# Row-wise exponentials on ScalarE in the transposed blocks of a matmul-logsumexp kernel

## The chip, the cores and the metric

The kernel runs on one core of one Trainium2 chip. The metric is the device time of one execution in microseconds (us). Engines are named as in the profile: PE is TensorE's matmul, PEld its weight load, DVE is VectorE, ACT is ScalarE, POOL is GpSimd. L382 means line 382 of the kernel that was profiled; inserted lines shift the numbers between kernels.

## The reference

```python
def setup_inputs():                    # m, k, n = 1024, 4096, 4096
    return {"a": np.random.randn(m, k).astype(np.float32),
            "b": np.random.randn(k, n).astype(np.float32)}

def reference(a, b):
    x = np.matmul(a, b)
    return special.logsumexp(x, axis=-1).astype(np.float32)
```

Only the 1024 results leave the chip. The product of a and b is reduced while it is still on the core.

## The kernel before

The columns of b are worked off in eight blocks of 512. Within a block, the kernel uses seven half-size products in place of eight (a Strassen scheme), so it also needs sums of quarters of b (`t1`, `t3`, `t4`, `t6`, `t7`, made on VectorE in fp16) and sums of result tiles. Blocks 3 to 6 are "transposed" (`wide` in the code): there b is the stationary operand, the columns of b lie on the partitions, and one matmul streams 512 rows of a. Each such block has two halves, and a half consists of seven products of 16 matmuls. Block 7, which follows, is not transposed.

In a transposed result tile the logsumexp has to go over partitions. So VectorE transposes the tile in squares of 32x32. Then each partition holds, for each of 16 groups, 32 values of one row of the result, with a maximum of its own. Before the change that maximum is subtracted by VectorE over the whole tile (a broadcast addition), one ScalarE instruction takes all 512 exponentials per partition, and VectorE sums them by group:

```python
    slots = [slots[:, 0:FD], slots[:, FD : 2 * FD]]      # two scratch tiles, 128x512 fp32
    blocks32 = lambda t: t.rearrange("p (c n) -> p c n", n=32)

    def lse_turned(c, slot, h, r):
        nm = tnm[:, 1 + h, ts(r, WN // 2)]
        v = blocks32(slot)
        nc.vector.transpose(out=slot, in_=c)
        nc.vector.tensor_reduce(out=nm, in_=v, axis=AX.X, op=ALU.max, negate=True)
        add(v, v, nm.unsqueeze(-1).broadcast_to((P, WN // 2, 32)))
        nc.scalar.activation(out=slot, in_=slot, func=AF.Exp)
        return lambda: nc.vector.tensor_reduce(
            out=tts[:, 1 + h, ts(r, WN // 2)], in_=v, axis=AX.X, op=ALU.add)

    def merge_turned():      # brings the groups' sums to one common maximum
        nc.vector.tensor_reduce(out=tmin, in_=tnm.rearrange("p a c -> p c a"), ...)
        sub(tnm, tnm, tmin...)
        nc.scalar.activation(out=tnm, in_=tnm, func=AF.Exp, scale=-1.0)
        # ... a multiplication, two additions and a copy on VectorE
```

One half of a transposed block, in program order. Each engine takes its own instructions in this order. `mk` makes sums of b for the next half; in the last half before block 7 (`last`) these sums are wider.

```python
            product(c11, ..., start=True)          # product 1
            product(c12, ..., start=True)          # product 2
            product(c21, ..., start=True)          # product 3
            flush()
            nc.vector.tensor_copy(out=s[:, 1], in_=c12)   # <- the c12 copy
            add(s[:, 1], s[:, 1], c21)
            sub(s[:, 0], s[:, 1], c11)
            for f in deferred:                     # previous half's sum of c11 and merge
                f()
            deferred.clear()
            mk("t1")
            product(c22, ..., start=True, stop=True)      # product 4
            mk("t6")
            mk("t3")
            product(c12, ..., stop=True)           # product 5 ADDS INTO c12
            sub(s[:, 0], c12, s[:, 0])
            add(c22, c22, s[:, 0])
            end12 = lse_turned(c12, slots[0], 1, 0)
            end22 = lse_turned(c22, slots[1], 1, 1)
            product(c21, ..., stop=True)           # product 6
            sub(s[:, 1], c21, s[:, 1])
            end12()
            end21 = lse_turned(c21, slots[0], 0, 1)
            end22()
            # ... mk("t4"), mk("t7")
            product(c11, ..., stop=True)           # product 7
            add(c11, c11, s[:, 1])
            e = fix_pool.tile([P, FD], f32, ...)
            end11 = lse_turned(c11, e, 0, 0)
            end21()
            # ... in the last half the rest of t4 and t7
            deferred.extend([end11, merge_turned])
```

A quad of block 7 (cut), which matters at the hand-over from the last transposed half:

```python
                m1(c11, start=True)
                m5(c12)
                nc.scalar.copy(out=e, in_=halves(r0))     # first copy of block 7
                m2(c21, start=True)
                m6(c22, start=final)
            nc.scalar.copy(out=s[:, 2], in_=c21)
            flush()
            # ... add, sub
            for f in deferred:                            # the merge of the last transposed half
                f()
            # ...
            m3(c12)                                       # adds into c12: waits for the first copy
            nc.scalar.copy(out=x[:, 0], in_=c12)
            m4(c21)
            nc.scalar.copy(out=x[:, 1], in_=c21)
            m7(c11)
```

## Time and profile before

| what | before |
|---|---|
| time, median of the first 6 runs | 427.2 us (426.86 to 428.54) |
| profiled span | 426.7 us |
| the eight transposed halves | 24.17 us each, TensorE never waits |
| TensorE's one long wait (hand-over to block 7) | 6.16 us |
| the 32 matmuls after it | 5.99 us, where full clock needs 3.49 |

The page's first two parts give the busy time of each engine over the whole span, then the busy share of each of 40 slices in tenths (a 9 is 90% or more). PEclk is the granted TensorE clock in tenths.

```profile
PE 413.9 (97%) x2747; PEld 261.7 (61%) x2747; DVE 338.4 (79%) x773; ACT 83.3 (20%) x191; POOL 79.1 (19%) x149
PE   8999999999999999999999999999999958999996
DVE  2556687888566648989999999999999997299955
ACT  2222250151142211101010110101010012222124
PEclk9999999999999999999999999999999996999999
```

TensorE is full but for one dip near the end (the 5 and the 8), and the clock drops in the slice of that dip's end (the 6). VectorE is nearly full in the transposed stage (147 to 340 us), ScalarE nearly idle.

The windows view gives the busy time of each engine in a stretch of time: one of the middle halves, the last half, then the wait at the hand-over, then the 32 matmuls after it.

```profile
core 0: us, PE busy (x) PEld busy (x) DVE busy (x) ACT busy (x) POOL busy (x), PEclk, DMA share, GB/s
243.93:268.10 24.17, 24.17 (x114) 10.96 (x112) 22.91 (x50) 2.80 (x5) 1.22 (x2) 1.00 1.03 171
316.45:340.60 24.15, 24.15 (x115) 10.96 (x113) 22.95 (x45) 1.54 (x3) 2.27 (x3) 1.00 0.03 4
347.45:353.61 6.16, 0.16 (x3) 0.00 (x0) 6.02 (x11) 1.16 (x3) 0.00 (x0) 0.87 1.24 207
353.61:359.60 5.99, 5.99 (x32) 4.43 (x32) 4.40 (x13) 0.77 (x3) 0.89 (x6) 0.57 1.24 207
```

In each half TensorE is busy throughout, while VectorE is busy for 22.9 of 24.17 us. It is near its limit but does not set the period. At the hand-over VectorE works without a gap while TensorE does nothing, and the matmuls after that run at a clock of 0.57 on the mean.

The waits view of TensorE from 147 to 362 us (what it waited for, and on whom; us in total, times, longest) has only this line, and the timeline of that moment (start, duration, and in brackets the idle time before and what ended it) shows why.

```profile
PE acc_0_0_3173 L528 <- ACT s_0_3175 L595: 6.0, 1, 6.0
```

```profile
351.67 0.69 DVE L86 TENSOR_TENSOR ew_1_3155<-ew_1_3155,ident 128x512 f32<-128x512 f32 x1
352.45 0.63 ACT L381 ACTIVATE ew_1_3155<-ew_1_3155 128x512 f32<-128x512 f32 x1 [5.24 <-DVE ew_1_3155 L86]
352.99 0.57 ACT L595 COPY s_0_3175<-acc_0_0_3173 128x512 f32<-128x512 f32 x1
```

ScalarE's copy of block 7's first tile (L595) stands behind the exponential of the last transposed tile (L381), which waits 5.24 us for VectorE's broadcast addition (L86). ScalarE itself is idle all that time, but it takes its instructions in order. The Trainium skill says the same of its queue ("TensorE: Matmul & The Clock Gate", the table at its head: eight deep, strict first in, first out), and this trace agrees with the order.

### The profile page before, as it was taken

How to read it: one execution, taken by the hardware profiler on the slowest of the kernel's cores; microseconds unless marked ns; L12 is line 12 of the kernel's file. 1: busy time of each engine (PE TensorE's matmuls, PEld its weight loads, DVE VectorE, ACT ScalarE, POOL GpSimd, SP SyncE). 2: the span in 40 equal slices, each digit the busy share in tenths (PEclk: the TensorE clock that was granted, in tenths of full speed). 3: DMA queues.
4: the chain of work that ended last, by engine and by line, in shares of the span. 5: the costliest groups of instructions: out<-in, count | busy, mean ns of one | idle time of the engine just before them, and what ended most of it. 6: DMA issues, size and time to landing. Idle time of an engine off the chain costs nothing.

```text
span 426.7 us, 6832 instructions
## 1 busy us (share of the span) xinstructions
PE 413.9 (97%) x2747; PEld 261.7 (61%) x2747; DVE 338.4 (79%) x773; ACT 83.3 (20%) x191; POOL 79.1 (19%) x149
## 2 busy tenths in 40 slices
PE   8999999999999999999999999999999958999996
PEld 3555568888888844444444444444444456888885
DVE  2556687888566648989999999999999997299955
ACT  2222250151142211101010110101010012222124
POOL 7667753001020200003000300003000203220000
PEclk9999999999999999999999999999999996999999
DMA  9999999999999299008930299007940199099100
GB/s 176 202 203 203 203 206 207 207 209 211 174 175 213 39 208 170 0 2 129 208 58 0 30 207 158 2 1 120 207 68 2 17 207 173 2 170 208 20 2 1
DMA packets 57840, 53.27 MB, mean 125 GB/s; under 512 B 10192, under 2 KB 56912, under 8 KB 57808
## 3 DMA queue, kind: packets, MB, share of 16 engines
q0 software_dynamic: 48928, 49.95, 71.0%
q1 hardware_dynamic: 8880, 2.89, 4.1%
q8 instruction: 21, 0.34, 0.3%
q14 instruction: 11, 0.09, 0.1%
HBM read 100.66 MB, written 2.10 MB: 241 GB/s over the span
## 4 chain that ended last, share of the span: by engine, by line
PE 88%; DVE 6%; DMA 4%; issue 0%; ACT 0%; POOL 0%; POOLq 0%; ACTq 0%
DMA tb<-in_a_dram 3%; PE acc_1_0_1347 L528 2%; PE acc_1_0_767 L528 2%; PE acc_0_0_765 L528 2%; PE acc_3_0_3755 L528 2%; PE acc_2_0_1482 L528 2%; PE acc_1_0_3307 L528 2%; PE acc_2_0_3483 L528 2%; PE acc_3_0_1615 L528 2%; PE acc_0_0_1215 L528 2%; PE acc_3_0_3619 L528 2%; PE acc_2_0_769 L528 2%; PE wide_0_2_2823 L427 2%; PE wide_1_0_2641 L427 2%; PE wide_0_1_2470 L427 2%; PE wide_1_2_2291 L427 2%
## 5 line engine op out<-in xcount | busy, mean ns | idle before, releaser
L528 PEld LDWEIGHTS <-aT 128*128 128x128 f16 x832 | 82.7, 99 | 16.9 <-issue 6.2
L427 PEld LDWEIGHTS <-tb 128*128 128x128 f16 x384 | 37.6, 98 | 45.1
L381 ACT ACTIVATE tb<-tb 128x512 f32<-128x512 f32 x24 | 15.1, 630 | 110.4 <-DVE tb L86 110.4
L205 POOL DMA_DIRECT2D tb<-in_a_dram x47 | 25.5, 546 | 6.6 <-issue 1.2
L227 DVE COPY aT<-tps_99 128x512 f16<-128x512 f16 x24 | 10.2, 425 | 19.7 <-PE tps_99 L216 19.7
L234 PEld LDWEIGHTS <-aT 128*128 128x128 f16 x192 | 16.7, 98 | 13.8 <-DVE aT L227 1.3
L216 PEld LDWEIGHTS <-tb 128*128 128x128 f16 x192 | 14.3, 99 | 14.6 <-DMA tb<-in_a_dram 5.9
L528 PEld LDWEIGHTS <-s_71 128*128 128x128 f16 x208 | 20.4, 98 | 2.8
L528 PEld LDWEIGHTS <-s_72 128*128 128x128 f16 x208 | 20.3, 98 | 2.4
L528 PEld LDWEIGHTS <-s_73 128*128 128x128 f16 x208 | 20.3, 98 | 2.4
L229 ACT COPY aT<-tps_100 128x512 f16<-128x512 f16 x24 | 14.1, 586 | 39.0 <-PE tps_100 L216 39.0
L86 DVE TENSOR_TENSOR tb<-tb,ident 128x512 f32<-128x512 f32 x24 | 16.6, 692 | 0.8
L379 DVE TENSOR_REDUCE ident<-tb 128x16 f32<-128x512 f32 x24 | 16.5, 686 | 0.9
L382 DVE TENSOR_REDUCE tts<-tb 128x16 f32<-128x512 f32 x24 | 16.3, 678 | 0.0
L89 DVE TENSOR_TENSOR aT<-aT 128x256 f16<-128x256 f16 (+1 forms) x56 | 16.2, 343 | 0.0
L86 DVE TENSOR_TENSOR s_71<-aT 128x256 f16<-128x256 f16 (+1 forms) x26 | 8.2, 317 | 3.2 <-ACT aT L229 2.2
L216 PE MATMUL tps_99<-ident,tb 128*128 128x128 f16 x96 | 9.5, 223 | 1.0 <-DMA tb<-in_a_dram 0.8
L216 PE MATMUL tps_100<-ident,tb 128*128 128x128 f16 x96 | 9.5, 223 | 0.0
L149 POOL DMA_DIRECT2D b_0_2813<-in_b_dram x1 | 0.9, 878 | 45.1 <-DVE tb L378 45.1
L149 POOL DMA_DIRECT2D b_0_3165<-in_b_dram x1 | 0.9, 878 | 44.5 <-DVE sw_1_2997 L89 44.5
L149 POOL DMA_DIRECT2D b_0_2461<-in_b_dram x1 | 0.9, 887 | 44.4 <-PE wide_1_0_2289 L427 44.4
L149 POOL DMA_DIRECT2D b_0_2109<-in_b_dram x1 | 0.9, 878 | 44.0 <-DVE tb L378 44.0
(905 smaller groups left out, 947.5 us busy)
## 6 DMA issues: line engine op xcount, KB each, us to landing
tb<-in_a_dram POOLq DMA_DIRECT2D x47, 128.0 KB, 5.9
aT<-in_b_dram POOLq DMA_DIRECT2D x4, 1024.0 KB, 15.2
b_1_86<-in_b_dram POOLq DMA_DIRECT2D x4, 256.0 KB, 6.6
b_2_87<-in_b_dram POOLq DMA_DIRECT2D x4, 256.0 KB, 6.2
b_3_88<-in_b_dram POOLq DMA_DIRECT2D x4, 256.0 KB, 6.2
b_0_89<-in_b_dram POOLq DMA_DIRECT2D x2, 512.0 KB, 8.6
b_1_90<-in_b_dram POOLq DMA_DIRECT2D x2, 512.0 KB, 11.8
b_2_91<-in_b_dram POOLq DMA_DIRECT2D x2, 512.0 KB, 15.2
```

The source lines that it names most:

```text
L86: nc.vector.tensor_tensor(out=o, in0=x, in1=y, op=ALU.add)
L89: nc.vector.tensor_tensor(out=o, in0=x, in1=y, op=ALU.subtract)
L205: nc.gpsimd.dma_start(out=slot, in_=a_m[m, :, k0 * P : (k0 + kn) * P])
L216: nc.tensor.matmul(pst[:, ts(j, P)], src[:, ts(j, P)], ident, is_transpose=True, start=(j == 0), stop=(j == kn - 1),)
L227: nc.vector.tensor_copy(out=dst, in_=v)
L229: nc.scalar.copy(out=dst, in_=v)
L234: nc.tensor.matmul(pt, aT[:, i, kp, m // 2, m % 2, :], blk0.raw[i // GI][:, i % GI, kp, :], start=(done[m] == 0), stop=(done[m] == KT - 1),)
L379: nc.vector.tensor_reduce(out=nm, in_=v, axis=AX.X, op=ALU.max, negate=True)
L381: nc.scalar.activation(out=slot, in_=slot, func=AF.Exp)
L382: return lambda: nc.vector.tensor_reduce(out=tts[:, 1 + h, ts(r, WN // 2)], in_=v, axis=AX.X, op=ALU.add)
L427: nc.tensor.matmul(c.rearrange("p (q m) -> p q m", m=P), lhs(i), rhs(i), start=(start and i == 0), stop=(stop and i == KP - 1), skip_group ...
L528: nc.tensor.matmul(c, lhs(i), rhs(i), start=(start and i == 0), stop=(i == KP - 1), skip_group_check=True,)
```

## The change

The intent is to move work from VectorE to ScalarE. For three of the four result tiles of a half, ScalarE takes the exponentials in 16 instructions of 128x32, each with its group's maximum as the bias and with its sum accumulated on the way. VectorE loses the broadcast addition and the sum of these tiles. ScalarE also takes over the c12 copy, and this copy now stands behind the deferred work of the previous half. Lastly, in the last half, the last two of the four groups of block 7's `t1`, `t6` and `t3` are made sooner: ahead of the deferred work and the c12 copy, at a point where VectorE would otherwise wait. Three tiles are done by rows in each half, but only two in the last. The core of the diff:

```diff
-    def lse_turned(c, slot, h, r):
+    def lse_turned(c, slot, h, r, by_rows=True):
         ...
+        if by_rows:
+            for i in range(WN // 2):               # 16
+                nc.scalar.activation(
+                    out=v[:, i], in_=v[:, i], func=AF.Exp,
+                    bias=nm[:, i : i + 1],
+                    accum_out=tts[:, 1 + h, r * WN // 2 + i : r * WN // 2 + i + 1],
+                )
+            return lambda: None
         add(v, v, nm.unsqueeze(-1).broadcast_to((P, WN // 2, 32)))
 ...  (merge_turned is cut in two: up to its exponential, and the rest)
-            flush()
-            nc.vector.tensor_copy(out=s[:, 1], in_=c12)
-            add(s[:, 1], s[:, 1], c21)
-            sub(s[:, 0], s[:, 1], c11)
+            if last:
+                for what in ("t1", "t6", "t3"):
+                    for g in range(G // 2, G):
+                        mk(what, g * GI, (g + 1) * GI)
             for f in deferred:
                 f()
             deferred.clear()
-            mk("t1")
+            flush()
+            nc.scalar.copy(out=s[:, 1], in_=c12)
+            add(s[:, 1], s[:, 1], c21)
+            sub(s[:, 0], s[:, 1], c11)
+            # mk("t1"), later "t6" and "t3": whole, or in the last half only groups 0 and 1
 ...
-            end22 = lse_turned(c22, slots[1], 1, 1)
+            end22 = lse_turned(c22, slots[1], 1, 1, not last)
 ...
-            end11 = lse_turned(c11, e, 0, 0)
+            end11 = lse_turned(c11, e, 0, 0, False)
```

More of the change, by code (lines that the diff above doesn't have):

```diff
@@ L379, in lse_turned @@
         nc.vector.tensor_reduce(out=nm, in_=v, axis=AX.X, op=ALU.max, negate=True)
+        if by_rows:
+            for i in range(WN // 2):
+                nc.scalar.activation(
+                    out=v[:, i],
+                    in_=v[:, i],
+                    func=AF.Exp,
+                    bias=nm[:, i : i + 1],
+                    accum_out=tts[:, 1 + h, r * WN // 2 + i : r * WN // 2 + i + 1],
+                )
+            return lambda: None
         add(v, v, nm.unsqueeze(-1).broadcast_to((P, WN // 2, 32)))
@@ L391, in merge_turned, with merge_turned_2 @@
         nc.scalar.activation(out=tnm, in_=tnm, func=AF.Exp, scale=-1.0)
+    def merge_turned_2():
         nc.vector.tensor_mul(out=tts, in0=tts, in1=tnm)
@@ L446, in wide_step @@
             deferred.clear()
-            mk("t1")
-            product(c22, lambda i: blk.T6[:, i], lambda i: aT[:, i, 0, :, 1], start=True, stop=True)
-            mk("t6")
-            mk("t3")
+            flush()
+            nc.scalar.copy(out=s[:, 1], in_=c12)
+            add(s[:, 1], s[:, 1], c21)
+            sub(s[:, 0], s[:, 1], c11)
+            if last:
+                for g in range(G // 2):
+                    mk("t1", g * GI, (g + 1) * GI)
+            else:
+                mk("t1")
+            product(c22, lambda i: blk.T6[:, i], lambda i: aT[:, i, 0, :, 1], start=True, stop=True)
+            for what in ("t6", "t3"):
+                if last:
+                    for g in range(G // 2):
+                        mk(what, g * GI, (g + 1) * GI)
+                else:
+                    mk(what)
             product(c12, lambda i: cols(i, 0, 1), lambda i: aT[:, i, 0, :, 0], stop=True)
@@ L475, in wide_step @@
                         mk(what, g * GI, (g + 1) * GI)
-            deferred.extend([end11, merge_turned])
+            deferred.extend([end11, merge_turned, merge_turned_2])
     blk, nxt = None, blk1
```

## The prediction

> **What bounds it now.** TensorE is busy 97% of 426.7 us. From 147 to 340 us (the eight transposed half-blocks) the chain of waits is TensorE alone: seven products of 3.45 us, 24.17 us per half. In the windows by half, VectorE is busy 22.9 of 24.17 us, ScalarE only 2.8. VectorE limits only the hand-over to block 7: the last half's sums are wider (0.60 us apart instead of 0.33), VectorE runs without a gap from 327 to 352 us, ScalarE's copy of block 7's first tile queues behind the last exponential, and TensorE stands still from 347.5 to 353.6 us (its longest wait, 6.0 us). The 32 matmuls after it take 6.16 us instead of 3.49 (granted clock 0.6 in that slice). So at most 6.1 + 2.7 = 8.8 us (2.1%) can be won.
>
> **What the change does.** VectorE loses, per half, three additions (0.61 us each), three sums (0.60) and one copy with its wait (1.07): about 4.7 us. ScalarE gains that copy (0.59) and 48 exponentials of 128x32, each with a pointer bias and an accumulator read. Cost of one, estimated: in the trace, accumulating 128x256 exponentials from PSUM start their read 357 ns after they start and the next starts 92 ns later; the one from SBUF (128x257) read after 415 ns. 32 columns take 187 ns less, so 212 + 92 = about 305 ns. The Trainium skill, "ScalarE: Activation LUTs", section "What ACT_TABLE_LOAD costs", gives 280 ns + 0.833 ns per column with 93 ns overlap: 214 ns before the read, which agrees. So 16 rows cost 4.9 us where one activation cost 0.63.
>
> **Where it lands.** Busy time would fit, but the order makes a ring. The c12 copy is now behind 48 row exponentials, the last 128x512 one, and the merge's exponential. The fifth product accumulates into c12, so it must wait for that copy. Following VectorE's order: copy, 1.4 us of additions, twelve sums (4.0), subtraction, addition, transposition, maximum (2.9), then 48 x 0.305 = 14.7 on ScalarE, then last exponential, sum, minimum, subtraction, exponential, copy (about 2.7): 25.7 us, against 24.17. Replaying the old order with trace durations reproduces TensorE's resumption at 353.6; the same for the new order gives waits of about 1.5 us before the fifth product from the fourth half on, in total about 9 us, and a hand-over wait of about 4.1 instead of 6.0 us (the early sums save VectorE 3.6 us just before it). Net +7 us, less perhaps 2.7 if the shorter wait leaves the clock high.
>
> **Prediction: 431.5 us, range 422 to 439. Chances: faster by over 2% 0.04, within 2% 0.78, slower by over 2% 0.18.** A ten-nanosecond error in the row pitch moves the result by 3.2 us; below 285 ns the ring is no longer the limit.
>
> **What would show it.** Right: row exponentials about 305 ns apart; TensorE waiting 1 to 2 us per half on ScalarE's copy (c12); half periods near 25.7 us; VectorE busy under 19 us per half, now idle for ScalarE; the hand-over wait 4 us. Wrong: half periods of 24.17 us with no wait on that copy (then about 421 to 424 us), or a hand-over wait that stays at 6 us.
>
> **What would make it wrong.** A shorter row pitch because small activations pipeline better, or a longer one because accumulator reads or instruction fetches add up; a clock that drops in the new waits.

## The result

The changed kernel takes **434.78 us** (median of 10 runs, 434.14 to 436.77). The kernel before, over the 20 runs beside it, takes 427.87 us (426.86 to 428.54). The ratio is 1.0171, with a 95% interval of 1.0158 to 1.0185. A ratio here and below is the mean time of one kernel's fast runs over that of the other's in the same rounds, so it is not quite the ratio of the medians that are quoted. The result lies in the predicted range and within 2%, but the loss is about 6.9 us where the prediction had 4.3.

The page of the changed kernel, the same parts as before:

```profile
PE 412.8 (95%) x2747; PEld 260.5 (60%) x2747; DVE 303.6 (70%) x719; ACT 184.9 (43%) x912; POOL 79.1 (18%) x149
PE   7999999999999999999898998989899896999996
DVE  2566687788457845696766769666697978299865
ACT  2222250151222315829376490946829273222124
PEclk9999999999999999999999999999999998999999
```

VectorE shed 35 us and ScalarE gained 102. TensorE, which had no gap in the transposed stage, now has 8s all through it. The dip at the end became milder, both in the PE row (a 5 and an 8 before, a single 6 after) and in PEclk (from 6 to 8).

The windows view, with columns as before: one of the middle halves, the last half, then the wait at the hand-over, then the 32 matmuls after it:

```profile
246.37:272.11 25.74, 24.33 (x113) 10.93 (x112) 18.45 (x42) 16.00 (x101) 1.22 (x2) 1.00 0.97 162
323.61:349.37 25.76, 24.17 (x113) 10.83 (x111) 22.02 (x43) 16.26 (x102) 2.13 (x3) 1.00 0.02 2
356.36:360.46 4.10, 0.16 (x3) 0.00 (x0) 4.00 (x8) 3.34 (x18) 0.00 (x0) 0.92 1.24 207
360.46:365.27 4.81, 4.81 (x33) 3.74 (x32) 3.73 (x12) 0.76 (x3) 0.36 (x3) 0.72 1.24 207
```

A half now takes 25.7 us although no engine but TensorE is busy for more than 18.5 of it (22.0 in the last). So no engine's load limits it, but a chain of dependences from engine to engine does. TensorE's waits from 147 to 362 us, the first lines:

```profile
PE acc_0_0_3472 L552 <- ACT s_0_3474 L619: 3.9, 1, 3.9
PE wide_1_1_3267 L439 <- DVE tts L86: 1.6, 1, 1.6
PE wide_1_1_2407 L439 <- DVE tts L86: 1.5, 1, 1.5
PE wide_0_1_3056 L439 <- DVE tts L86: 1.4, 1, 1.4
...
```

There is one wait per half from the third half on, each time before the first matmul of the fifth product (tile `wide_..._1` is c12). The timeline of one of them shows the end of the chain:

```profile
310.09 0.31 ACT L382 ACTIVATE tb<-tb,ident 128x32 f32<-128x32 f32 x1
310.30 0.19 ACT L382 ACTIVATION_READ_ACCUMULATOR tb<-tb,ident 128x1 f32 x1
310.40 0.62 ACT L391 ACTIVATE ew_1_3042<-ew_1_3042 128x512 f32<-128x512 f32 x1
311.05 0.69 DVE L392 TENSOR_REDUCE tts<-ew_1_3042 128x16 f32<-128x512 f32 x1 [3.35 <-ACT ew_1_3042 L391]
...
312.29 0.28 ACT L401 ACTIVATE ident<-ident 128x96 f32<-128x96 f32 x1 [1.27 <-DVE ident L89]
312.47 0.57 ACT L460 COPY sw_0_3059<-wide_0_1_3056 128x512 f32<-128x512 f32 x1
...
313.09 0.38 PE L439 MATMUL wide_0_1_3056<-aT,b_0_2617 128*128 128x512 f16 x1 [1.42 <-DVE tts L86]
```

From the top: the last row exponential of c21 and its accumulator read; the exponential of c11 (L391); VectorE, which has waited 3.35 us for it, sums it (L392); the minimum and the subtraction of the merge (left out); the merge's exponential (L401); the copy of c12 (L460), ending at 313.04; and the fifth product, at 313.09. The waits view names a VectorE addition (L86) as releaser. But the trace's own record of this matmul has it wait for the counter that ScalarE's instructions raise, that is, for the copy, and experiment e1 below bears this out. The profile infers releasers from what ended nearest in time, and here it took the wrong one.

### The profile page after: what moved, and what is told of

The parts are those of the page before. It is cut to its first block, busy times and chain, and to the rows that moved or that the text cites. A ratio compares the mean times of both kernels' runs of the same rounds, so it can differ in the third digit from the quotient of the medians.

```text
span 432.3 us, 7514 instructions
## 1 busy us (share of the span) xinstructions
PE 412.8 (95%) x2747; PEld 260.5 (60%) x2747; DVE 303.6 (70%) x719; ACT 184.9 (43%) x912; POOL 79.1 (18%) x149
## 4 chain that ended last, share of the span: by engine, by line
PE 47%; DVE 25%; ACT 20%; DMA 6%; issue 1%; POOL 0%; ACTq 0%; POOLq 0%; DVEq 0%
ACT tb L382 18%; DVE tb L86 5%; DMA tb<-in_a_dram 4%; DVE ident L379 3%; DVE tb L378 3%; DVE tb L89 2%; PE acc_1_0_1347 L552 2%; PE acc_1_0_767 L552 2%; PE acc_2_0_769 L552 2%; PE acc_3_0_3918 L552 2%; PE acc_3_0_4054 L552 2%; PE acc_3_0_1615 L552 2%; PE acc_0_0_1215 L552 2%; PE acc_2_0_3782 L552 2%; PE acc_1_0_3606 L552 2%; PE acc_2_0_1482 L552 2%
## 5 line engine op out<-in xcount | busy, mean ns | idle before, releaser
L382 ACT ACTIVATE tb<-tb,ident 128x32 f32<-128x32 f32 x368 | 112.2, 307 | 72.6 <-DVE ident L379 72.6
L382 ACT ACTIVATION_READ_ACCUMULATOR tb<-tb,ident 128x1 f32 x368 | 69.0, 187 | 0.0
L86 DVE TENSOR_TENSOR s_71<-aT 128x256 f16<-128x256 f16 (+1 forms) x26 | 8.2, 316 | 1.8 <-ACT aT L229 1.5
L86 DVE TENSOR_TENSOR s_73<-aT 128x256 f16<-128x256 f16 (+1 forms) x26 | 8.3, 317 | 0.0
```

The source lines that it names most:

```text
L86: nc.vector.tensor_tensor(out=o, in0=x, in1=y, op=ALU.add)
L382: nc.scalar.activation(out=v[:, i], in_=v[:, i], func=AF.Exp, bias=nm[:, i : i + 1], accum_out=tts[:, 1 + h, r * WN // 2 + i : r * WN // 2 ...
```

## How the time divides

Profile against profile, from the start of the transposed stage to the end of the kernel:

| term | predicted | measured |
|---|---|---|
| eight halves: 193.39 to 202.89 us | about +9 | +9.50 |
| hand-over wait: 6.16 to 4.10 us | -1.9 | -2.06 |
| the 32 matmuls after it: 5.99 to 4.81 us | -2.7 | -1.19 (-0.84 in the control f1) |
| sum | +4.3 | +6.26 |

The third line is the one that failed. The part of the kernel before the stage differs between the profiles by up to about 1 us (146.22 to 147.19 us), for code that the edits don't touch, and the median of the kernel before moved from 427.2 to 427.87 us with more runs. So medians (+6.9) and profiles (+6.26) agree only that far.

## The theories

The ring theory is the prediction's. Copy of c12, two additions, twelve sums of b, a subtraction, an addition, a transposition and a maximum on VectorE, 48 row exponentials at 0.305 us on ScalarE, the last exponential, its sum, the merge up to its exponential, and the next half's copy of c12 form a ring. Its length is about 25.7 us, longer than TensorE's 24.17, because the copy was put on ScalarE behind all of this.

The load theory is the first rival: ScalarE's exponentials, or the shared memory accesses of the busier engines, slow the half wherever the copy stands.

For the hand-over the clock theory is: the wait itself costs little beyond its length, and if it gets shorter, the clock stays at full speed. The rival is that any wait of this size lowers the clock, and that behind the wait another one is hidden.

## Experiments

Diffs are against the changed kernel unless said otherwise. "Wait before the fifth product" is the sum, over the eight halves, of what a half takes beyond 24.17 us; "hand-over wait" is the time from one matmul's start to the next one's, less the 0.11 us that it is at full pace. Both are therefore 0.16 us longer for each wait than the idle time in the waits view, which begins at the modelled end of a matmul. "Left" marks what is left of the wait behind the idle matmuls; "the 32 matmuls" take 3.49 us at full clock without waits. Of f3 and g2, which are edits of the kernel before, the numbers are put beside that kernel's.

| kernel | transposed half, us | wait before 5th product | hand-over wait | the 32 matmuls | median, us | ratio to before |
|---|---|---|---|---|---|---|
| before | 24.17 | 0 | 6.16 | 5.99 | 427.87 | 1 |
| after | 25.54 to 25.92 from the third on | 9.5 | 4.10 | 4.81 | 434.78 | 1.0171 |
| e1 copy on VectorE | 24.17, last 24.67 | 0.5 | 6.20 | 5.95 | 428.44 | 1.0015 [0.999, 1.0041] |
| e2 c12 whole | 24.17 | 0 | 1.53 | 3.77 | 420.94 | 0.9843 [0.9824, 0.9863] |
| e3 c12 whole, last exp late | 24.17 | 0 | 0.13 | 5.16 | 421.13 | 0.9851 [0.983, 0.9871] |
| e4 no accumulation | 24.17, last 26.25 | 2.08 | 3.34 | 5.16 | 426.03 | 0.996 [0.9938, 0.9981] |
| f1 after again | as after | as after | 4.10 | 5.16 | 434.56 | 1.0163 [1.0134, 1.0192] |
| f2 after, idle matmuls | as after | as after | 0.61 left | 3.76 | 434.55 | 1.0158 [1.0127, 1.0188] |
| f3 before, idle matmuls | 24.17 | 0 | 0.91 left | 4.36 | 426.37 | 0.9969 [0.9944, 0.9994] |
| f4 no early sums | as after | as after | 7.71 | 4.79 | 438.75 | 1.0257 [1.0229, 1.0286] |
| g1 best | 24.17 | 0 | 0.12 | 3.49 | 419.8 | 0.9817 [0.98, 0.9833] |
| g2 f3 and merge late | 24.17 | 0 | 0.90 left | 3.49 | 425.73 | 0.9959 [0.9941, 0.9977] |
| g3 f2 and merge late | as after | as after | 0.60 left | 3.49 | 433.02 | 1.0128 [1.0113, 1.0143] |
| g4 no rows | 24.17, last 24.78 | 0.6 | 3.81 | 6.23 | 426.45 | 0.9963 [0.9941, 0.9985] |

### e1: the copy back to VectorE and, with its two additions, ahead of the merge

```diff
+            flush()
+            nc.vector.tensor_copy(out=s[:, 1], in_=c12)
+            add(s[:, 1], s[:, 1], c21)
+            sub(s[:, 0], s[:, 1], c11)
             for f in deferred:
                 f()
             deferred.clear()
-            flush()
-            nc.scalar.copy(out=s[:, 1], in_=c12)
-            add(s[:, 1], s[:, 1], c21)
-            sub(s[:, 0], s[:, 1], c11)
```

> The changed kernel with only the c12 copy put back on VectorE, ahead of the merge, as it was before; the row exponentials stay on ScalarE. Theory (ring through ScalarE's queue: copy behind 48 row exponentials): the wait before the fifth product goes, half periods return to 24.17 us although ScalarE is as busy as before (about 16 us per half); the hand-over wait is about 5.9 us; time near the kernel before, 427 to 429 us. Rival (the row exponentials themselves are too much for ScalarE, wherever the copy sits): half periods stay near 25.7 us and the time near 434 us.

The time is 428.44 us. The windows view of a half in the middle, then TensorE's waits:

```profile
242.20:266.40 24.20, 24.20 (x114) 10.94 (x112) 18.92 (x44) 15.31 (x99) 2.56 (x3) 1.00 1.06 174
```

```profile
PE acc L552 <- ACT s L619: 6.0, 1, 6.0
PE wide L439 <- DVE sw L457: 0.3, 1, 0.3
```

ScalarE still takes 48 row exponentials per half and is busy for 15.3 us, but the half takes 24.2 us again. The load theory has fallen, and the ring theory stands: the copy's place costs the 9 us. (Its engine and its position were changed together; which of the two would be enough was not tested.) The merge's VectorE additions (L86 in the waits of after) come even later than the copy in e1, and yet the fifth product waits for nobody, save 0.5 us in the last half. So it was not they that it had waited for. The hand-over wait went back to 6.2 us, 2.1 us more than in the changed kernel. Of these, 1.25 us are only that TensorE is no longer held up in the last half and so is done with it earlier (24.67 us against 25.92); the other 0.85 us are that VectorE, counted from the start of that half, takes up the last c21 tile later (29.43 us against 28.58). So a part of what the change gains at the hand-over is a wait that it has moved into the half before. (The profiled span is 0.74 us longer in its tail than before's; this is not explained.)

### e2: c12 as before, whole; c21 and c22 by rows

```diff
-            end12 = lse_turned(c12, slots[0], 1, 0)
+            end12 = lse_turned(c12, slots[0], 1, 0, False)
```

> The changed kernel with only the first of the three turned tiles (c12) going back to one addition, one whole exponential and one sum. Theory: the ring loses 4.9 - 0.6 us, falls below 24.17 us, so no wait before the fifth product; the hand-over wait falls from 3.9 to about 1.4 us; 423 us, or 420 to 421 us if the clock stays high. Rival (merging before the copy, or the early sums, make the waits): half periods stay above 25 us, time above 430 us.

The time is 420.94 us, 1.6% below the kernel before. TensorE's waits from 147 to 362 us are a single line, the hand-over:

```profile
PE acc L552 <- ACT s L619: 1.4, 1, 1.4
```

The ring has 32 row exponentials in place of 48: 16 x 0.305 = 4.9 us go from it, and one exponential of 0.63 us, with an addition and a sum on VectorE of 0.7 us each, comes in. That is enough, and TensorE doesn't wait in any half. The hand-over wait is down to 1.53 us, and the clock stays at 1.0. The remaining 0.28 us beyond 3.49 is a wait for a copy.

### e3: e2, and the last tile's exponential behind block 7's first copies

`lse_turned` gets `late`, and then issues its activation together with its sum, in the deferred part:

```diff
+        if late:
+            return lambda: (
+                nc.scalar.activation(out=slot, in_=slot, func=AF.Exp),
+                sums(),
+            )
...
-            end11 = lse_turned(c11, e, 0, 0, False)
+            end11 = lse_turned(c11, e, 0, 0, False, last)
```

> As the run before, and in the last half the exponential of c11 is issued behind block 7's two first copies on ScalarE. Theory (the hand-over wait is ScalarE's queue order, copies behind the last exponential): hand-over wait about 0, clock stays high, 419 to 420 us. Rival (block 7 waits for VectorE's sums themselves): the wait moves to another product and the time stays near that of the run before.

The time is 421.13 us, the same as e2, so the expectation was missed. The hand-over wait did go (0.13 us), but block 7's seventh product waits in its stead. The waits view, then the timeline:

```profile
PE acc L558 <- ACT s L700: 1.5, 1, 1.5
```

```profile
351.90 0.26 DVE L89 TENSOR_TENSOR ident<-ident,tmin 128x96 f32<-128x96 f32 x1
352.25 0.28 ACT L407 ACTIVATE ident<-ident 128x96 f32<-128x96 f32 x1 [3.59 <-DVE ident L89]
352.44 0.35 ACT L700 COPY s<-acc 128x256 f32<-128x256 f32 x1
352.85 0.60 PE L558 MATMUL acc<-b,aT 128*128 128x256 f16 x4 [1.50 <-ACT s L700]
```

The copy (L700) stands behind the merge's small exponential (L407), which waits for VectorE. It is the same pattern one instruction later, and it was hidden as long as the first wait was there. This is the second wait of the rival theory.

### e4: rows without the accumulation

```diff
                     bias=nm[:, i : i + 1],
-                    accum_out=tts[:, 1 + h, ...],
                 )
-            return lambda: None
+            return lambda: nc.vector.tensor_reduce(..., axis=AX.X, op=ALU.add)
```

> The changed kernel with row exponentials that take the bias but do not accumulate; VectorE makes the three sums as before. Theory (the ring's length is 48 row pitches plus 11 us): row pitch 213 ns instead of 305, ring about 21.3 us, so half periods 24.17 us (the last one about 25.6, VectorE having more to do); hand-over wait about 3.2 us; 425 to 427 us. Rival (it is the number of instructions or the position of the copy alone): half periods stay above 25 us, time 432 us or more.

The time is 426.03 us. The row exponentials now start 212 ns apart (median), against 305 ns with the accumulator read. So the read costs 93 ns per instruction in the chain, 4.5 us for 48 of them, and without it TensorE doesn't wait in seven of eight halves. (The last took 26.25 us where 25.6 were expected; the expectation puts that down to VectorE, which has more to do there. No run tests it.) The group's line of each kernel (count, busy time, mean ns of one) shows that the single instruction is no shorter, first after, then e4:

```profile
L382 ACT ACTIVATE tb<-tb,ident 128x32 f32<-128x32 f32 x368 | 112.2, 307 | 72.6 <-DVE ident L379 72.6
```

```profile
L382 ACT ACTIVATE tb<-tb,ident 128x32 f32<-128x32 f32 x368 | 79.0, 306 | 73.2 <-DVE ident L379 73.2
```

The mean is 307 and 306 ns. In e4 the instructions overlap, which is why their busy time is 79.0 us and not 112.2. The Trainium skill ("ScalarE: Activation LUTs", What ACT_TABLE_LOAD costs) gives 280 ns plus 0.833 ns per column for an activation with a pointer bias, and 93 ns of overlap; an estimate from that is 307 ns alone and 214 ns in a row. The trace agrees with both, at 306 and 212.

### f1: the changed kernel once more, as a control

> The changed kernel unchanged, as the control of this call: ratio to the kernel before near 1.017, about 434.8 us.

The time is 434.56 us, with one run of 435.77 us at a mean clock of 0.992 where the others have 0.995 or 0.996. The hand-over wait is 4.10 us again; the 32 matmuls after it took 5.16 us where the first profile had 4.81:

```profile
360.60:365.76 5.16, 5.16 (x32) 4.00 (x32) 3.74 (x12) 0.77 (x3) 0.66 (x5) 0.67 1.24 207
```

### f2 and f3: idle matmuls in the hand-over wait

A matmul into a tile that nobody reads keeps TensorE busy without changing anything else. f2 puts 32 of them into the wait of the changed kernel, f3 puts 48 into that of the kernel before:

```diff
                 m6(c22, start=final)
+            if early and q == 0:
+                idle = psum_pool.tile([P, FD], f32, name="idle", tag="ps")[:, 0:H]
+                for _ in range(2):          # f3: range(3)
+                    m5(idle, start=True)
```

> The changed kernel with two products (32 matmuls, 3.5 us) into a bank that nobody reads, placed in TensorE's hand-over wait of 3.9 us. Theory (the predicted time was too low because the shorter wait still lowers the clock; only about 1.2 of the 2.7 us came back): the 32 matmuls after the wait take 3.5 us instead of 5.0, granted clock full in that slice, time 1.0 to 1.5 us below the control. Rival (the excess over the prediction sits elsewhere, in a longer ring): time within 0.4 us of the control.

> The kernel before with three such products (48 matmuls, 5.2 us) in its hand-over wait of 6.0 us. Theory: the 32 matmuls after the wait take 3.5 instead of 6.2 us; time 2.7 us lower, about 425.2 us. Rival (the slow matmuls after the wait have another cause than TensorE's idleness): they stay at 6.2 us and the time at 427.9 us.

The windows view of f2, the wait and the 32 matmuls, to be laid beside the last two lines of after's:

```profile
356.14:360.24 4.10, 3.65 (x34) 3.12 (x32) 4.00 (x8) 3.34 (x18) 0.00 (x0) 1.00 1.25 208
360.24:364.00 3.76, 3.65 (x33) 3.13 (x32) 3.26 (x9) 0.82 (x4) 0.00 (x0) 1.00 1.24 207
```

The wait has the same length, but the clock is 1.00 in both stretches, and the 32 matmuls take 3.76 us. From the stage's start on, this profile is 1.45 us shorter than the control's. Yet the timed runs spread from 432.83 to 436.1 us, all at a clock of 0.998 or more, and their median is that of the control. So the expected gain of 1.0 to 1.5 us did not show in the time, and there f2 is inconclusive. A part of the spread lies outside the core's span: two runs (434.76 and 435.06 us) are 2.9 to 3.3 us longer than their spans, where the others and all of the control are 1.7 to 1.9 us longer. By the median of the spans f2 is about 0.65 us shorter than the control (432.15 against 432.8 us). The rest of the spread at full clock stays open.

f3 took 426.37 us, a gain of about 1.3 us on the median of the kernel before, where 2.7 was expected. Its waits say what ate the rest:

```profile
PE acc L528 <- ACT s L595: 0.8, 1, 0.8
PE acc L528 <- ACT s L674: 0.7, 1, 0.7
```

With the clock at full speed the matmuls reach the seventh product sooner and wait there for a copy (L674), again behind the merge's exponential. So of the 2.5 us by which the 32 matmuls exceeded 3.49 in the kernel before, a fast clock alone could win only 1.6 (down to 4.36): the second wait was hidden beneath the slow clock.

### f4: the early sums taken back

```diff
-            if last:
-                for what in ("t1", "t6", "t3"):
-                    for g in range(G // 2, G):
-                        mk(what, g * GI, (g + 1) * GI)
...
+            mk("t1")
+            for what in ("t6", "t3"):
+                mk(what)
```

> The changed kernel with block 7's sums of the second half back in their old place. Theory (the early sums fill VectorE's wait for ScalarE and take 3.6 us out of the hand-over): hand-over wait about 7.5 us instead of 3.9, half periods as in the control, time 3.5 to 4.8 us above the control. Rival (early sums delay the merge and lengthen the last half): time equal to or below the control.

The time is 438.75 us, 4.2 us above the control, and the hand-over wait is 7.71 us (7.5 in the waits view):

```profile
PE wide L439 <- DVE tts L86: 8.3, 6, 1.5
PE acc L540 <- ACT s L607: 7.5, 1, 7.5
```

So the early sums are worth 3.6 us of wait, and the whole gain of the change at the hand-over comes from them and not from the rows alone. In the profiled run the 32 matmuls took 4.79 us, no more than after a wait of 4.1 us: a longer wait needn't mean a longer loss to the clock. But this run is the fastest of the six (437.5 us). Four of the others have a mean clock of 0.988 and took 438.57 to 440.17 us, so they lost more to it, and a part of the 4.2 us is probably clock.

### g1: the version that the experiments point to

e3, and in block 7's first quad the merge goes behind the next two copies:

```diff
             sub(s[:, 0], s[:, 2], e[:, 0])
+            behind_copies = []
+            if early and q == 0:
+                behind_copies, deferred = deferred[1:], deferred[:1]
             for f in deferred:
                 f()
...
             nc.scalar.copy(out=x[:, 1], in_=c21)
             m7(c11)
+            for f in behind_copies:
+                f()
```

> The run with c12 whole and the last exponential behind block 7's first copies, and now also the merge (its minimum, exponential and sums) behind block 7's next two copies on ScalarE. Theory (in that run the wait did not vanish but moved: block 7's seventh product waited 1.5 us for a copy that stood behind the merge's exponential): that wait falls to about 0.3 us (the copy still waits for one subtraction on VectorE), time about 1.2 us lower, 419.6 to 420.2 us. Rival (block 7's product waits for VectorE's sums): the wait stays at 1.5 us.

The time is **419.8 us** (419.44 to 420.26), a ratio of 0.9817 to the kernel before, with correct results. The copies (L703, L705) now come out ahead of the merge's exponential (L407), and the waits view has no line left for TensorE between 147 and 362 us. ScalarE's timeline there, and the page:

```profile
350.14 0.37 ACT L703 COPY s<-acc 128x256 f32<-128x256 f32 x1 [2.06 <-DVE s L86]
350.80 0.37 ACT L705 COPY s<-acc 128x256 f32<-128x256 f32 x1 [0.28 <-PE acc L558]
351.61 0.28 ACT L407 ACTIVATE ident<-ident 128x96 f32<-128x96 f32 x1 [0.44 <-DVE ident L89]
```

```profile
PE 410.4 (98%) x2747; PEld 260.2 (62%) x2747; DVE 314.3 (75%) x735; ACT 151.0 (36%) x664; POOL 78.9 (19%) x149
```

### g2 and g3: f3 and f2 with the merge moved as in g1

The edit is that of g1 added to f3 (the kernel before) and to f2 (the changed kernel).

> The kernel before with 48 idle matmuls in its hand-over wait and the merge behind block 7's copies. Theory (of the 2.5 us that the slow clock cost the kernel before, only 1.6 came back because the copy behind the merge's exponential was the next limit): the 32 matmuls after the wait take 3.5 us instead of 4.4 with idle matmuls alone and 6.0 without; 2.5 us below the kernel before, 425.1 to 425.5 us. Rival (the idle matmuls do not bring the whole clock back): they stay at 4.4 us.

> The changed kernel with 32 idle matmuls in its hand-over wait and the merge behind block 7's copies. Theory: the 32 matmuls after the wait take 3.5 us where the control took 5.2 and idle matmuls alone gave 3.8; about 1.6 us below the control, 432.9 to 433.3 us. Rival: no change in time against idle matmuls alone, 434.5 us.

They were run at other times. They took 425.73 us (0.2 us above what was expected) and 433.02 us, with the 32 matmuls at 3.49 us in both. So a fast clock and no second wait together bring 1.8 us to the kernel before (427.49) and, to the changed kernel, 1.5 us on the control (by ratios, 1.0128 against 1.0163; the two intervals still touch, so the size of this gain is uncertain). For the changed kernel this is the part of the predicted credit that it does not get by itself. These two also tell that the hand-over explains only a small part of the loss: g3 is still 1.3% slower than before, by its ring.

### g4: none of the tiles by rows

```diff
-            end12 = lse_turned(c12, slots[0], 1, 0)
-            end22 = lse_turned(c22, slots[1], 1, 1, not last)
+            end12 = lse_turned(c12, slots[0], 1, 0, False)
+            end22 = lse_turned(c22, slots[1], 1, 1, False)
...
-            end21 = lse_turned(c21, slots[0], 0, 1)
+            end21 = lse_turned(c21, slots[0], 0, 1, False)
```

> The changed kernel with no row exponentials at all: the copy on ScalarE, the merge first and the early sums stay. Theory: no ring, half periods 24.17 us except a little more in the last, hand-over wait about 3.6 us, 424 to 426 us, so above the run with c12 whole (420.9 us): two tiles by rows are worth 3 to 4 us, three cost 10. Rival (row exponentials only ever cost): equal to or below 420.9 us.

The time is 426.45 us. Without any rows, the copy on ScalarE and the early sums bring 0.4%. e2, which differs only by c21 and c22 in rows, brings 1.6%. It was run at another time. So two tiles in rows are worth about 1.2% (some 5 us, where 3 to 4 were expected). This is where they act: the hand-over wait is 3.81 us in g4 and 1.53 in e2, the 32 matmuls 6.23 and 3.77. One run of g4 had a mean clock of 0.998 and took 424.6 us; the other three had 0.992 and took 426.3 to 426.87. So within one kernel the clock at the hand-over is worth about 2 us.

### What the clock does at the hand-over

The Trainium skill ("TensorE: Matmul & The Clock Gate", Part 1: The HAM clock gate) says that the clock is halved after at least one idle window of 3413 ns, that the windows run freely, and that a busy window releases it. The clock record of the traces agrees in the length: half-clock intervals last 3.41 us or 6.83 us, one window or two. In the kernel before, it was two windows, of which 5.2 us ran matmuls (2.5 us lost); in the profile of after it was one, 2.7 us of it with matmuls (1.3 lost, and 1.7 in f1). The window need not be idle, however. On a grid of 3.413 us laid through the record's changes, windows in which TensorE was busy for 22% (f1) and 23% (g4) lowered the clock, and one with 39% (e4, in its last half) did not, nor did those of about 50% at the changed kernel's waits before the fifth product. In the half-clock state windows with 48% (e1), 52% (before) and 66% (g4) didn't release it, and ones with 79% (f4) and 80% (after) did. So, by these figures, how many windows are lost depends on how the wait lies on the grid. The waits of after, 4.1 us, gave one window in most runs (mean clock 0.995 or 0.996) and two in a few (0.992: 435.77, 435.94 and 436.77 us), but full clock never. The kernel before had two in nearly all runs (0.991 or 0.992); two of its runs, at 0.995, took 426.5 and 426.76 us, about 1 us less than its median. That a mean clock of 0.995 is one window and 0.992 two is read from the profiled runs, which alone have a record of the windows. By the same reading f4's runs at 0.988 had three, and one run each of e4 and g4, at 0.998, had none.

## Why the prediction was right or wrong, point by point

- **The ring.** "Half periods near 25.7 us", and TensorE waiting on ScalarE's copy of c12: right. The halves measured 25.54 to 25.92 us, the waits 1.37 to 1.75 us each. They set in from the third half, not from the fourth: six waits with a sum of 9.5 us where the prediction had "about 9". (Its own words, 1.5 us each from the fourth half on, give only 7.5.) e1 shows the cause to be the place of the copy, e2 and e4 show that the ring's length decides.
- **The row pitch of "about 305 ns".** Right: 305 ns. Both parts are confirmed by e4: 212 ns without the read, 93 ns for the read. The working given for the 212 does not carry it, though: 187 ns less than its traced 357 and 415 ns is 170 and 228. Only the estimate of 214 ns that it sets beside this, with the 92 ns to the next start added, comes to about 306. Nor does "below 285 ns the ring is no longer the limit" follow: 25.7 less 24.17 us over 48 rows is 32 ns, so about 273. No run had a pitch between 212 and 305 ns.
- **"VectorE busy under 19 us per half".** Right (18.45 us), save in the last half (22.02 us).
- **The hand-over wait, "about 4.1 instead of 6.0 us (the early sums save VectorE 3.6 us just before it)".** Right: 4.10 us (3.9 in the waits view, where before has 6.0), and f4 gives 3.6 us for the early sums.
- **"Net +7 us, less perhaps 2.7 if the shorter wait leaves the clock high".** This is the step that failed. The net of about 7 us was right, but 431.5 us counted the credit of 2.7 us in full, and it measured 1.19 us (0.84 in the control). Two things were wrong in it. First, a wait of 4.1 us lowered the clock in every run here, usually for one window and sometimes for two; I had taken its being shorter for its being short enough. Second, even a clock that stays high would not have given the whole credit, as the seventh product then meets the copy behind the merge's exponential on ScalarE: with the clock at 1.00 the 32 matmuls still took 3.76 us in the changed kernel (f2), and 4.36 in the kernel before (f3), and came to 3.49 only when the merge was moved too (g2, g3). The term was a possibility and should have been entered by its chance, or costed by asking how long the wait must be for the clock to stay. The prediction also gave 6.16 us for the 32 matmuls, which is what the windows view has for the wait; they took 5.99.
- **"At most 6.1 + 2.7 = 8.8 us (2.1%) can be won".** Close: g1 removes the whole wait, the clock loss and the second wait without any loss in the halves, and is 7.7 us (1.8%) below the kernel before, or 8.55 us from profile to profile, counted from the stage's start.
- **The rest of the miss.** The forecast was +4.3 us; the medians give +6.9. The clock credit accounts for 1.5, the ring's larger sum for 0.5. The remainder, about 0.6 us, is of the size by which unchanged code before the stage differs between runs, and isn't explained further.

## What to carry to other kernels

When work moves to an idle engine, walk the chain of dependences around one period, with that engine's strict order in it, and compare its length with the period; the busy shares say nothing about it, and one copy that frees a tile for the next matmul should never stand behind work that waits for another engine. A gain that hangs on the clock staying high is to be entered by its chance, since a TensorE wait of some 4 us already cost one or two windows of half clock here and one of 1.5 us cost none. Before a wait's whole length is booked as a gain, look for the next wait behind it: here two small exponentials on ScalarE each held up a copy, and only taking out both (g1) gave the full gain.

## What the Trainium skill lacked or had wrong

- "ScalarE: Activation LUTs", What ACT_TABLE_LOAD costs, gives the cost of an activation but none for accumulating its sum. Here the accumulator read adds 93 ns from start to start: 305 ns against 212 for 128x32 with a pointer bias. Many small accumulating activations so cost 1.44 times what they cost without it.
- "TensorE: Matmul & The Clock Gate", Part 1, says that the clock drops after an idle window. Here windows with TensorE busy for 22 and 23% lowered it and one with 39% did not; and for the release, 79 and 80% sufficed and 48 to 66% did not. The window's length, 3.41 us, agrees. No page has these shares.
- The same part does not say how many windows a wait of a given length costs. Here the half clock lasts whole windows (3.41 or 6.83 us) whatever the wait's length: in the profiled runs waits of 3.3 and 4.1 us cost one window, of 3.8 and 6.2 us two, and one of 7.7 us two, of which only 2.7 us were felt by matmuls. By their mean clock other runs of the same kernels had more or fewer.
